# Second feed-forward input of a float32 decoder step: every second gate/up pair by seven half-token block products

## The chip, the core and the metric

The kernel runs as one program on one core of a Trainium2 chip. The metric is the device time of one execution in microseconds (us). TensorE (PE, with its weight loads as PEld), VectorE (DVE), ScalarE (ACT), GpSimd (POOL) and SyncE (SP, which issues the weight transfers) run side by side and wait for each other by semaphores.

## The reference

One layer of a hybrid recurrent decoder over 256 prompt tokens, 64 sample tokens and 16 meta tokens: a feed-forward block (FFN1), a token mixer with gated linear scans, and a second feed-forward block (FFN2). The part that matters here, cut from the reference:

```python
def swiglu(h, norm_w, w_in, w_out):
    u = rmsnorm(h, norm_w)
    g, up = jnp.split(u @ w_in, 2, axis=-1)      # w_in: 2048 x 11264
    return (jax.nn.silu(g) * up) @ w_out         # w_out: 5632 x 2048
...
    h = h + 0.5 * swiglu(h, ffn2_norm[l], w_ffn2_in[l], w_ffn2_out[l])
return rmsnorm(h, final_norm), ...
```

In FFN2 the meta tokens are gone: 320 tokens (`NO`) go through it.

## The kernel before

Activations lie transposed: 128 features in the partitions, tokens along the free dimension, `KT` = 16 feature tiles. Every large product is made of float32 numbers split in two parts: `uh` and `ul` (high and low part of the normalised input), and for each weight unit a high part `a` and a low part `b`. A unit is a 128x1024 piece of weights, eight 128x128 blocks. `stage` loads it (SP), casts it to the high part (ACT) and subtracts to get the low part (DVE); `mm3` then issues three matmuls for each block, a by uh, a by ul, b by uh, each over all 320 tokens into one PSUM bank. The high parts live in three buffers (`whp`), the low parts in three (`wlp`), the raw units in four (`rawp`), so that the staging of a unit waits for the matmuls of the unit three before it.

FFN2 (`ffn("f2", ...)`) has 44 gate/up pairs in 4 groups of 11. For one pair, `gin` calls `proj` twice (gate, up: 2 units, 48 matmuls each), then scales both by the norm factor `R`, applies the sigmoid and splits the product in `hh`, `hl`. `gout` multiplies a finished group by its part of `w_out`: 16 output tiles of two units (768 and 640 columns, 33 matmuls), each added to `h` by one DVE instruction. The order is that of the code, a group's `gin` and then the `gout` of the group before it; a scheduler then fixes one instruction order for each engine ahead of time, and each engine works through its own list in that order.

Of the kernel before, what the change touches and what calls it, by code (L numbers as in the profile page):

```python
# [20 lines left out]
NO = SEQ + NS  # L21
NT = NO + META
# [44 lines left out]
V_ALL = 100  # L67


def hybrid_step(tc, xT, w1i, w1a, w1b, win, wal, wup, wou, w2i, w2a, w2b, vec, cst_in, s0a, s0b,  # L70
                y, spa, spb, ssa, ssb):
    nc = tc.nc
    ctx = ExitStack()
    with ctx:
# [23 lines left out]
        def bank(tag, name, bufs):  # L98
            return psm.tile([P, 512], F32, tag=tag, name=name, bufs=bufs)

        def mmbank(name):
            return bank("mm", name, 3)

        def scbank(name):
            return bank("sc", name, 3)

        def stage(src, cols, name):
            r = rawp.tile([P, UNIT], F32, tag="raw", name="r" + name)
            nc.sync.dma_start(r[:, :cols], src)
# [157 lines left out]
        with ExitStack() as mx:  # L267
# [416 lines left out]
                advance()  # L684
            outpass(3, enter(V_N2, NO))

        def leave(m):
# [116 lines left out]
```

## Time and profile before

| | |
|---|---|
| time of three runs | 2563.48, 2564.34 (median), 2565.23 us |
| profiled execution, first to last instruction (span) | 2562.7 us |
| median less span | 1.6 us |
| PE, DVE, ACT busy over the span | 99%, 55%, 41% |
| FFN2 on PE: first matmul at 1617.77 us, the closing norm at 2547.57 us | 929.8 us |

A matmul's record is longer than the distance to the next, since matmuls are pipelined; how often PE starts one is read from the start times or from a stretch and its count. `idle before ... <-X` names what ended a wait.

### The profile page before, as it was taken

How to read it: one execution, taken by the hardware profiler on the slowest of the kernel's cores; microseconds unless marked ns; L12 is line 12 of the kernel's file. 1: busy time of each engine (PE TensorE's matmuls, PEld its weight loads, DVE VectorE, ACT ScalarE, POOL GpSimd, SP SyncE). 2: the span in 40 equal slices, each digit the busy share in tenths (PEclk: the TensorE clock that was granted, in tenths of full speed). 3: DMA queues.
4: the chain of work that ended last, by engine and by line, in shares of the span. 5: the costliest groups of instructions: out<-in, count | busy, mean ns of one | idle time of the engine just before them, and what ended most of it. 6: DMA issues, size and time to landing. Idle time of an engine off the chain costs nothing.

```text
span 2562.7 us, 43617 instructions
## 1 busy us (share of the span) xinstructions
PE 2539.0 (99%) x18086; PEld 2512.0 (98%) x18086; DVE 1421.3 (55%) x2395; ACT 1063.1 (41%) x1573; POOL 33.2 (1%) x65
## 2 busy tenths in 40 slices
PE   9999999999999999999999999999999999999997
PEld 8999999999999999999999999999999999999997
DVE  6454444444444456866757778655454554455454
ACT  6333333333333346555455456533333333333334
POOL 0000000000000000000000000000000000000000
PEclk9999999999999999999999999999999999999999
DMA  6444445444544444454444543544444544544453
GB/s 205 145 141 142 145 130 158 143 134 139 156 144 130 142 146 151 152 166 158 159 149 128 165 143 110 172 149 148 150 144 143 165 148 136 164 153 149 134 152 126
DMA packets 120247, 378.78 MB, mean 148 GB/s; under 512 B 13648, under 2 KB 16720, under 8 KB 120048
## 3 DMA queue, kind: packets, MB, share of 16 engines
q1 hardware_dynamic: 114176, 357.34, 45.5%
q0 software_dynamic: 5184, 17.83, 1.9%
q8 instruction: 141, 2.31, 0.4%
q10 hardware_dynamic: 688, 0.82, 0.1%
q14 instruction: 58, 0.48, 0.1%
HBM read 363.88 MB, written 12.06 MB: 147 GB/s over the span
## 4 chain that ended last, share of the span: by engine, by line
PE 59%; issue 38%; ACT 1%; DVE 1%; DMA 0%; SPq 0%; POOL 0%; POOLq 0%
PE po L124 4%; PE po L126 4%; PE po L125 4%; PE pf1u L125 4%; PE pf1g L125 4%; PE pf1g L124 4%; PE pf1u L124 4%; PE pf1g L126 4%; PE pf1u L126 4%; PE pw L124 1%; PE pw L125 1%; PE pw L126 1%; PE kv L505 1%; PE A L424 0%; PE st L124 0%
## 5 line engine op out<-in xcount | busy, mean ns | idle before, releaser
L125 PE MATMUL pf2u<-ul,af2u 128*128 128x320 f32 x704 | 218.3, 310 | 0.0
L125 PE MATMUL pf2g<-ul,af2g 128*128 128x320 f32 x704 | 218.3, 310 | 0.0
L124 PE MATMUL pf2u<-uh,af2u 128*128 128x320 f32 x704 | 217.5, 309 | 0.0
L124 PE MATMUL pf2g<-uh,af2g 128*128 128x320 f32 x704 | 217.3, 309 | 0.0
L126 PE MATMUL pf2u<-uh,bf2u 128*128 128x320 f32 x704 | 216.8, 308 | 0.0
L126 PE MATMUL pf2g<-uh,bf2g 128*128 128x320 f32 x704 | 216.8, 308 | 0.0
L124 PE MATMUL pf1g<-uh,af1g 128*128 128x336 f32 x672 | 212.9, 317 | 0.0
L125 PE MATMUL pf1u<-ul,af1u 128*128 128x336 f32 x672 | 212.8, 317 | 0.0
L125 PE MATMUL pf1g<-ul,af1g 128*128 128x336 f32 x672 | 212.8, 317 | 0.0
L124 PE MATMUL pf1u<-uh,af1u 128*128 128x336 f32 x672 | 212.7, 316 | 0.0
L126 PE MATMUL pf1g<-uh,bf1g 128*128 128x336 f32 x672 | 211.8, 315 | 0.0
L126 PE MATMUL pf1u<-uh,bf1u 128*128 128x336 f32 x672 | 211.8, 315 | 0.0
L111 ACT CAST af2g<-rf2g 128x1024 fp32r<-128x1024 f32 x88 | 92.3, 1049 | 192.9 <-PE pf2g L125 101.5
L111 ACT CAST af2u<-rf2u 128x1024 fp32r<-128x1024 f32 x88 | 92.3, 1049 | 184.2 <-PE pf2u L125 96.1
L111 ACT CAST af1g<-rf1g 128x1024 fp32r<-128x1024 f32 x84 | 88.1, 1048 | 193.7 <-PE pf1g L125 100.6
L111 ACT CAST af1u<-rf1u 128x1024 fp32r<-128x1024 f32 x84 | 88.1, 1049 | 192.3 <-PE pf1u L125 103.0
L113 DVE TENSOR_TENSOR bf2g<-rf2g,af2g 128x1024 fp32r<-128x1024 f32 x88 | 107.9, 1226 | 102.3 <-ACT af2g L111 102.3
L113 DVE TENSOR_TENSOR bf1g<-rf1g,af1g 128x1024 fp32r<-128x1024 f32 x84 | 103.0, 1226 | 100.6 <-ACT af1g L111 100.6
L113 DVE TENSOR_TENSOR bf2u<-rf2u,af2u 128x1024 fp32r<-128x1024 f32 x88 | 107.9, 1226 | 83.0 <-ACT af2u L111 83.0
L113 DVE TENSOR_TENSOR bf1u<-rf1u,af1u 128x1024 fp32r<-128x1024 f32 x84 | 103.0, 1226 | 87.9 <-ACT af1u L111 87.9
L126 PEld LDWEIGHTS pf2g<-uh,bf2g 128*128 128x128 f32 x704 | 132.5, 188 | 0.0
L126 PEld LDWEIGHTS pf2u<-uh,bf2u 128*128 128x128 f32 x704 | 132.5, 188 | 0.0
(1140 smaller groups left out, 7338.8 us busy)
## 6 DMA issues: line engine op xcount, KB each, us to landing
rf2g<-i_w2i SPq DMA_DIRECT2D x88, 512.0 KB, 3.6
rf2u<-i_w2i SPq DMA_DIRECT2D x88, 512.0 KB, 3.6
rf1g<-i_w1i SPq DMA_DIRECT2D x84, 512.0 KB, 3.6
rf1u<-i_w1i SPq DMA_DIRECT2D x84, 512.0 KB, 3.6
rw<-i_wou SPq DMA_DIRECT2D x32, 320.0 KB, 2.9
rw<-i_wou SPq DMA_DIRECT2D x12, 512.0 KB, 3.6
s<-i_s0a POOLq DMA_DIRECT2D x8, 512.0 KB, 4.8
s<-i_s0b POOLq DMA_DIRECT2D x8, 512.0 KB, 4.9
```

The costliest lines, as they stand in the source:

```text
L111: nc.scalar.copy(a[:, :cols], r[:, :cols])
L113: nc.vector.tensor_tensor(out=b[:, :cols], in0=r[:, :cols], in1=a[:, :cols].bitcast(F32), op=ALU.subtract)
L124: nc.tensor.matmul(ps, a[:, s], xh, start=(first and k == 0), stop=False)
L125: nc.tensor.matmul(ps, a[:, s], xl, start=False, stop=False)
L126: nc.tensor.matmul(ps, b[:, s], xh, start=False, stop=(last and k == n - 1))
L505: nc.tensor.matmul(kv, kk, vv, start=True, stop=True)
```

## The change

FFN2 gets a function of its own, `ffn2`, in place of `ffn`. 23 of the 44 pairs stay as they were (`plain`: the same 96 matmuls). The 21 odd pairs from 3 on (`SEVEN`) are computed by Strassen's algorithm on 2x2 blocks. The blocks of the input are even or odd feature tiles by first or second half of the tokens (160 each, `HO`), the blocks of the weights are gate or up by even or odd feature tiles, and seven products of sums of blocks take the place of eight products of blocks. Each product is eight times a matmul of `a` with high and low part of a half side by side (2 x 160 columns) and a matmul of `b` with the high part alone (160 columns). To allow that, `uh` and `ul` become interleaved halves of one tile `uhl`. `transform` makes the sums of input blocks (T0 to T3) once at the start of FFN2; `seven` loads four raw units r11, r12, r21, r22, forms the sums of weights on DVE, and collects the products in `m1`, `z`, `m7` and the PSUM tile `pa`. `raw` gives r21 and r22 two buffers of their own ("sraw", one each). `w_ffn2_in` is laid out on the host by even and odd tiles, `w_ffn2_out` by seven groups of 6, 6, 6, 6, 6, 7, 7 hidden tiles, and `gout` of the group before is now spread between the pairs, as one unit of 768 or 896 columns for an output tile.

```diff
+HO = NO // 2
+GROUPS2 = (6, 6, 6, 6, 6, 7, 7)
+GAT2 = [sum(GROUPS2[:g]) for g in range(len(GROUPS2) + 1)]
+SEVEN = {m for m in range(3, FT) if m % 2}
...
-        uh = cst.tile([P, KT, NT], F32R, name="uh")
-        ul = cst.tile([P, KT, NT], F32R, name="ul")
+        uhl = cst.tile([P, KT, 2, NT], F32R, name="uhl")
+        uh = uhl[:, :, 0]
+        ul = uhl[:, :, 1]
...
+        def ffn2(after):
...
+                def transform(i):
+                    e, o = 2 * i, 2 * i + 1
+                    we, wo = (v[:, V_N2 + k:V_N2 + k + 1] for k in (e, o))
+                    ta, tb, tc_ = (tmp.tile([P, NT], F32, tag=t, name="tf") for t in ("t0", "t1", "t2"))
+                    nc.vector.tensor_tensor(out=ta[:, t0], in0=h[:, e, t0], in1=h[:, e, t1], op=ALU.subtract)
+                    nc.scalar.activation(ta[:, t1], ta[:, t0], AF.Identity, scale=we)
+                    nc.scalar.activation(tc_[:, t0], h[:, o, t1], AF.Identity, scale=wo)
...
+                    for d, src, sg in ((0, ta[:, t1], 1.0), (1, tb[:, t0], -1.0), (3, tb[:, t1], -1.0),
+                                       (2, tc_[:, t1], -1.0)):
+                        nc.scalar.activation(T[d][:, i, 0], src, AF.Copy, scale=sg)
+                        nc.vector.scalar_tensor_tensor(out=T[d][:, i, 1], in0=src, scalar=sg,
+                                                       in1=T[d][:, i, 0].bitcast(F32), op0=ALU.mult, op1=ALU.subtract)
+
+                def cut(r, name):
+                    a = whp.tile([P, UNIT], F32R, tag="wh", name="a" + name)
+                    nc.scalar.copy(a, r)
+                    b = wlp.tile([P, UNIT], F32R, tag="wl", name="b" + name)
+                    nc.vector.tensor_tensor(out=b, in0=r, in1=a.bitcast(F32), op=ALU.subtract)
+                    return a, b
...
+                def prod(ps, ab, x, first, last):
+                    a, b = ab
+                    po = ps.rearrange("p (a t) -> p a t", a=2)
+                    for i in range(KT // 2):
+                        s = slice(i * P, (i + 1) * P)
+                        xi = x(i)
+                        nc.tensor.matmul(po, a[:, s], xi, start=(first and i == 0), stop=False, skip_group_check=True)
+                        nc.tensor.matmul(ps[:, t0], b[:, s], xi[:, 0], start=False, stop=(last and i == KT // 2 - 1), skip_group_check=True)
...
+                def seven(m, gs, us):
...
+                    r11 = raw(w2i[m, 0], "s11", rawp, "raw", 4)
+                    pa = bank("o", "pa", 2)[:, :NO]
+                    prod(pa, cut(r11, "s11"), B(0, t0), True, False)
+                    m1 = fac.tile([P, NO], F32, tag="m1", name="m1")
+                    nc.scalar.copy(m1, pa)
+                    r12 = raw(w2i[m, 1], "s12", rawp, "raw", 4)
+                    pb = scbank("pb")[:, :NO]
+                    prod(pb, cut(r12, "s12"), B(1, t0), True, True)
+                    nc.vector.tensor_tensor(out=m1, in0=pb, in1=m1, op=ALU.add)
+                    fold(gs[:, t0], m1)
+                    r21 = raw(w2i[m + 1, 0], "s21", fac, "sraw", 2)
+                    r22 = raw(w2i[m + 1, 1], "s22", fac, "sraw", 2)
+                    p1 = fac.tile([P, UNIT], F32, tag="sum", name="p1")
+                    nc.vector.tensor_tensor(out=p1, in0=r21, in1=r22, op=ALU.add)
+                    nc.vector.tensor_tensor(out=r21, in0=r21, in1=r11, op=ALU.add)
+                    nc.vector.tensor_tensor(out=r11, in0=p1, in1=r11, op=ALU.add)
+                    prod(pa, cut(r11, "s2"), X(1), False, False)
+                    z = fac.tile([P, NO], F32, tag="z", name="z")
+                    nc.scalar.copy(z, pa)
+                    pc = scbank("pc")[:, :NO]
+                    prod(pc, cut(r21, "s3"), X(2), True, False)
+                    m7 = fac.tile([P, NO], F32, tag="m7", name="m7")
+                    nc.scalar.copy(m7, pc)
+                    prod(pa, cut(p1, "s1"), X(0), False, False)
+                    nc.vector.tensor_tensor(out=m7, in0=pa, in1=m7, op=ALU.add)
+                    fold(us[:, t1], m7)
+                    prod(pc, cut(r22, "s22"), X(3), False, True)
+                    nc.vector.tensor_tensor(out=z, in0=pc, in1=z, op=ALU.add)
+                    fold(us[:, t0], z)
+                    nc.vector.tensor_tensor(out=r12, in0=r11, in1=r12, op=ALU.add)
+                    prod(pa, cut(r12, "s4"), B(1, t1), False, True)
+                    nc.vector.tensor_reduce(out=gs[:, t1], in_=pa.rearrange("p (a t) -> p t a", a=2), axis=AX.X,
+                                            op=ALU.add)
...
+                for g, n in enumerate(GROUPS2):
+                    for j in range(n):
+                        gin(g, j)
+                        if g == 0 and j < 2:
+                            for i in range(4 * j, 4 * j + 4):
+                                transform(i)
+                        if g:
+                            for m in range(KT * j // n, KT * (j + 1) // n):
+                                gout(g - 1, m)
+                for m in range(KT):
+                    gout(len(GROUPS2) - 1, m)
...
-        ffn("f2", w2i, w2a, w2b, NO, leave, None)
+        ffn2(leave)
```

The seven products of one pair are called here by the names of their weights, in the order in which PE makes them: s11, s12, s2, s3, s1, s22, s4.

**How it moves PE.** Before, PE's list within a gate tile of FFN2 reads as follows (`pf2g` is the PSUM tile, `af2g` and `bf2g` the two parts of the unit):

```order
L124 MATMUL pf2g_19408<-uh,af2g_0_19398 128x320
L125 MATMUL pf2g_19408<-ul,af2g_0_19398 128x320
L126 MATMUL pf2g_19408<-uh,bf2g_0_19400 128x320
L124 MATMUL pf2g_19408<-uh,af2g_0_19398 128x320
L125 MATMUL pf2g_19408<-ul,af2g_0_19398 128x320
L126 MATMUL pf2g_19408<-uh,bf2g_0_19400 128x320
```

In the changed kernel, the end of product s22 (into `pc`) and the start of s4 (into `pa`) of one pair of `SEVEN` read:

```order
L736 MATMUL pc_20264<-T3_17148,as22_20309 128x320
L737 MATMUL pc_20264<-T3_17148,bs22_20311 128x160
L736 MATMUL pc_20264<-T3_17148,as22_20309 128x320
L737 MATMUL pc_20264<-T3_17148,bs22_20311 128x160
L736 MATMUL pa_20186<-uhl_74,as4_20332 128x320 [waits DVE_49]
L737 MATMUL pa_20186<-uhl_74,bs4_20334 128x160
```

Three matmuls of 320 columns for a block of weights have become one of 320 and one of 160, 112 for a pair where there were 96, each with a weight block of its own; and s4 begins with a wait for DVE.

**How it moves DVE and SP.** On DVE, in the second half of a pair of `SEVEN`, there stands (`bs22`, `bs4` are the low parts that `cut` makes, `p1_20238` is the first sum of the next pair of `SEVEN`, made of its `rs21` and `rs22`, and `m7` reads `pa` once s1 is in it):

```order
L722 TENSOR_TENSOR bs22_19844<-rs22_19769,as22_19842 128x1024 [waits PE_49,Activation_49]
L722 TENSOR_TENSOR bs4_19867<-rs12_19742,as4_19865 128x1024 [waits PE_49,Activation_49]
L758 TENSOR_TENSOR p1_20238<-rs21_20234,rs22_20236 128x1024 [waits DMAHW6_49,DMAHW5_49,DVE_49]
L769 TENSOR_TENSOR m7_19818<-pa_19719,m7_19818 128x320 [waits PE_49,Activation_49]
L118 TENSOR_TENSOR bf2o1_2_19898<-rf2o1_2_19894,af2o1_2_19896 128x768 [waits DMAHW2_49,Activation_49]
L740 TENSOR_TENSOR us_19716<-m7_19818 128x160 [waits DVE_49]
L772 TENSOR_TENSOR z_19795<-pc_19797,z_19795 128x320 [waits PE_49]
```

On SP the two raw units of the next pair, `rs21` and `rs22`, stand among the loads that follow, each behind a wait for DVE:

```order
L114 DMA rf2o1_8_20361<-i_w2o 128x768 [waits DMAHW4_49,DVE_49]
L114 DMA rf2o1_9_20387<-i_w2o 128x768 [waits DMAHW5_49,DVE_49]
L114 DMA rf2g32_0_20416<-i_w2i 128x1024 [waits DVE_49]
L727 DMA rs21_20675<-i_w2i 128x1024 [waits DVE_49]
L727 DMA rs22_20677<-i_w2i 128x1024 [waits DVE_49]
L114 DMA rf2g32_1_20446<-i_w2i 128x1024 [waits DVE_49]
```

In the code, `p1` of the next pair comes more than a whole `plain` pair later than `m7`; the scheduler has put it ahead of `m7`. It does so in 20 of the 21 pairs (the last has no next). Before the change no DVE instruction of FFN2 used a unit that had not been cast by ACT first.

**How it moves DVE at the start of FFN2.** Between the first pairs DVE now makes the eight transforms; ahead of the third pair's first low part (`bf2g_0_17563`) there stand:

```order
L704 TENSOR_TENSOR tf<-h 128x160
L710 SCALAR_TENSOR_TENSOR tf<-h,v,tf 128x160 [waits Activation_49]
L803 TENSOR_TENSOR gs<-pf2g_17358,R 128x320 [waits DVE_49,PE_49]
L707 TENSOR_TENSOR tf<-tf 128x160 [waits Activation_49]
L715 SCALAR_TENSOR_TENSOR T_17147<-tf,T_17147 128x160 [waits Activation_49]
L708 SCALAR_TENSOR_TENSOR tf<-h,v,tf 128x160 [waits DVE_49]
L715 SCALAR_TENSOR_TENSOR T_17145<-tf,T_17145 128x160 [waits Activation_49]
L715 SCALAR_TENSOR_TENSOR T_17146<-tf,T_17146 128x160 [waits Activation_49]
L806 TENSOR_TENSOR gs<-gs,sg 128x320
L704 TENSOR_TENSOR tf<-h 128x160 [waits DVE_49]
L118 TENSOR_TENSOR bf2g_0_17563<-rf2g_0_17559,af2g_0_17561 128x1024 [waits DMAHW2_49]
```

Fourteen more instructions of 160 columns stand directly ahead of these, since the second pair's last low part; before the change the low part of the next unit followed there after two instructions of 320 columns at most.

## Rows read from the trace of the kernel before

**Rows 1.** The page: busy time, granted clock by slice, chain that ended last

```profile
span 2562.7 us, 43617 instructions
PE 2539.0 (99%) x18086; PEld 2512.0 (98%) x18086; DVE 1421.3 (55%) x2395; ACT 1063.1 (41%) x1573; POOL 33.2 (1%) x65
...
PEclk9999999999999999999999999999999999999999
...
PE 59%; issue 38%; ACT 1%; DVE 1%; DMA 0%; SPq 0%; POOL 0%; POOLq 0%
```

**Rows 2.** Busy time by engine in the stretch of FFN2

```profile
core 0: us, PE busy (x) PEld busy (x) DVE busy (x) ACT busy (x) POOL busy (x), PEclk, DMA share, GB/s
1617.77:2547.57 929.80, 929.80 (x6341) 929.64 (x6340) 465.22 (x606) 340.31 (x429) 0.00 (x0) 1.00 0.48 147
```

**Rows 3.** Waits in FFN2: who waited for whom, total us, times, longest

```profile
DVE bf2g L113 <- ACT af2g L111: 101.8, 86, 2.3
ACT af2g L111 <- PE pf2g L125: 101.5, 41, 2.5
```

**Rows 4.** Timeline (start us, length us): PE restarts after a wait, then runs steadily

```profile
1569.41 0.19 PEld L124 LDWEIGHTS pw<-oh,aw 128*128 128x128 f32 x1 [2.07 <-DVE h L670]
1569.41 0.42 PE L124 MATMUL pw<-oh,aw 128*128 128x320 f32 x1 [1.83 <-DVE h L670]
1569.52 0.19 PEld L125 LDWEIGHTS pw<-ol,aw 128*128 128x128 f32 x1
1569.67 0.31 PE L125 MATMUL pw<-ol,aw 128*128 128x320 f32 x1
1569.67 0.19 PEld L126 LDWEIGHTS pw<-oh,bw 128*128 128x128 f32 x1
1569.82 0.31 PE L126 MATMUL pw<-oh,bw 128*128 128x320 f32 x1
```

**Rows 5.** Weight loads by shape, whole span: busy us, mean ns of one

```profile
L126 PEld LDWEIGHTS pf2g<-uh,bf2g 128*128 128x128 f32 x704 | 132.5, 188 | 0.0
L424 PEld LDWEIGHTS A<-Q,K 128*32 128x32 f32 x960 | 12.8, 109 | 1.1 <-ACT ktok L415 1.0
```

**Rows 6.** DVE in FFN2 by line: busy us, mean ns of one, idle before

```profile
L113 DVE TENSOR_TENSOR bf2g<-rf2g,af2g 128x1024 fp32r<-128x1024 f32 x87 | 106.7, 1226 | 101.8 <-ACT af2g L111 101.8
L206 DVE SCALAR_TENSOR_TENSOR h<-po,h 128x320 f32<-128x320 f32 x63 | 31.0, 492 | 46.4 <-PE po L126 46.3
L141 DVE TENSOR_TENSOR hl<-us,hh 128x320 fp32r<-128x320 f32 x44 | 21.4, 486 | 0.0
L113 DVE TENSOR_TENSOR bf2o_9a<-rf2o_9a,af2o_9a 128x768 fp32r<-128x768 f32 x4 | 3.8, 958 | 0.9 <-ACT af2o_9a L111 0.9
```

**Rows 7.** ACT in FFN2 by line

```profile
L111 ACT CAST af2u<-rf2u 128x1024 fp32r<-128x1024 f32 x88 | 92.3, 1049 | 184.2 <-PE pf2u L125 96.1 <-PE pf2g L125 81.1 <-PE pf2u L126 2.8
L193 ACT ACTIVATE sg<-gs 128x320 f32<-128x320 f32 x44 | 20.6, 467 | 0.0
```

**Rows 8.** The raw units of the gate tiles: transfers and their time to landing

```profile
L109 SPq DMA_DIRECT2D rf2g<-i_w2i x88: 327/328/328, 1606.3 to 2363.4; - x88
...
DMA to landing us min/median/max: 3.3/3.6/5.1
```

**Rows 9.** Timeline of FFN2: hand-overs from PE to ACT, and from DVE to SP

```profile
1801.05 0.31 PE L125 MATMUL pf2u<-ul,af2u 128*128 128x320 f32 x1
...
1801.44 1.05 ACT L111 CAST af2u<-rf2u 128x1024 fp32r<-128x1024 f32 x1 [2.47 <-PE pf2u L125]
...
1802.52 1.23 DVE L113 TENSOR_TENSOR bf2u<-rf2u,af2u 128x1024 fp32r<-128x1024 f32 x1
...
1803.78 0.33 SPq L109 DMA_DIRECT2D rf2u<-i_w2i  x1
```

More of the change, by code (lines that the diff above doesn't have):

```diff
@@ L685, in hybrid_step, with raw, fold, plain @@
             outpass(3, enter(V_N2, NO))
+        def ffn2(after):
+            with ExitStack() as fx:
+                hidp = fx.enter_context(tc.tile_pool(name="hid2", bufs=2))
+                fac = fx.enter_context(tc.tile_pool(name="fac", bufs=1))
+                T = [fac.tile([P, KT // 2, 2, HO], F32R, name=f"T{i}") for i in range(4)]
+                hid = {}
+                t0, t1 = slice(0, HO), slice(HO, NO)
+                def transform(i):
[5 more added lines that the diff above has]
+                    nc.scalar.activation(tc_[:, t0], h[:, o, t1], AF.Identity, scale=wo)
+                    nc.vector.tensor_tensor(out=tb[:, t0], in0=tc_[:, t0], in1=ta[:, t1], op=ALU.add)
+                    nc.vector.scalar_tensor_tensor(out=tb[:, t1], in0=h[:, o, t0], scalar=wo, in1=tb[:, t0],
+                                                   op0=ALU.mult, op1=ALU.subtract)
+                    nc.vector.scalar_tensor_tensor(out=tc_[:, t1], in0=h[:, e, t1], scalar=we, in1=tc_[:, t0],
+                                                   op0=ALU.mult, op1=ALU.subtract)
+                    for d, src, sg in ((0, ta[:, t1], 1.0), (1, tb[:, t0], -1.0), (3, tb[:, t1], -1.0),
[9 more added lines that the diff above has]
+                    return a, b
+                def raw(src, name, pool, tag, bufs):
+                    r = pool.tile([P, UNIT], F32, tag=tag, name="r" + name, bufs=bufs)
+                    nc.sync.dma_start(r, src)
+                    return r
+                def prod(ps, ab, x, first, last):
[6 more added lines that the diff above has]
+                        nc.tensor.matmul(ps[:, t0], b[:, s], xi[:, 0], start=False, stop=(last and i == KT // 2 - 1), skip_group_check=True)
+                def fold(out, x):
+                    nc.vector.tensor_tensor(out=out, in0=x[:, t0], in1=x[:, t1], op=ALU.add)
+                def seven(m, gs, us):
+                    B = lambda q, t: (lambda i: uhl[:, 2 * i + q, :, t])
+                    X = lambda d: (lambda i: T[d][:, i])
+                    r11 = raw(w2i[m, 0], "s11", rawp, "raw", 4)
[31 more added lines that the diff above has]
+                                            op=ALU.add)
+                def plain(m, name):
+                    ps = mmbank("p" + name)[:, :NO]
+                    for q in range(2):
+                        un = stage(w2i[m, q], UNIT, f"{name}_{q}")
+                        mm3(ps, [(*un, 0, 8)], [(uh[:, k, :NO], ul[:, k, :NO]) for k in range(q, KT, 2)],
+                            first=(q == 0), last=(q == 1))
+                    return ps
+                def gin(g, j):
+                    if j == 0:
+                        hid[g] = [hidp.tile([P, max(GROUPS2), NO], F32R, tag=t, name=t) for t in ("hh", "hl")]
+                    jj = GAT2[g] + j
+                    gs = tmp.tile([P, NT], F32, tag="t0", name="gs")[:, :NO]
+                    us = tmp.tile([P, NT], F32, tag="t2", name="us")[:, :NO]
+                    sign = 1.0
+                    if jj in SEVEN:
+                        seven(2 * jj, gs, us)
+                        pg, pu, sign = gs, us, -1.0
+                    else:
+                        pg = plain(2 * jj, f"f2g{2 * jj}")
+                        if jj == 0:
+                            rstd(NO)
+                        pu = plain(2 * jj + 1, f"f2u{2 * jj}")
+                    sg = tmp.tile([P, NT], F32, tag="t1", name="sg")[:, :NO]
+                    nc.vector.tensor_tensor(out=gs, in0=pg, in1=R[:, :NO], op=ALU.mult)
+                    nc.scalar.activation(sg, gs, AF.Sigmoid)
+                    nc.vector.tensor_tensor(out=us, in0=pu, in1=R[:, :NO], op=ALU.mult)
+                    nc.vector.tensor_tensor(out=gs, in0=gs, in1=sg, op=ALU.mult)
+                    if sign > 0:
+                        nc.vector.tensor_tensor(out=us, in0=us, in1=gs, op=ALU.mult)
+                    else:
+                        nc.vector.scalar_tensor_tensor(out=us, in0=us, scalar=sign, in1=gs, op0=ALU.mult,
+                                                       op1=ALU.mult)
+                    hh, hl = hid[g]
+                    split(hh[:, j], hl[:, j], us)
+                def gout(g, m):
+                    n = GROUPS2[g]
+                    hh, hl = hid[g]
+                    at = KT * P * P * GAT2[g] + m * P * P * n
+                    un = stage(w2o[at:at + P * P * n].rearrange("(p c) -> p c", p=P), n * P, f"f2o{g}_{m}")
+                    ps = mmbank("po")[:, :NO]
+                    mm3(ps, [(*un, 0, n)], [(hh[:, j], hl[:, j]) for j in range(n)])
+                    nc.vector.scalar_tensor_tensor(out=h[:, m, :NO], in0=ps, scalar=0.5, in1=h[:, m, :NO],
+                                                   op0=ALU.mult, op1=ALU.add)
+                    if g == len(GROUPS2) - 1:
+                        after(m)
+                for g, n in enumerate(GROUPS2):
[9 more added lines that the diff above has]
+                    gout(len(GROUPS2) - 1, m)
@@ L769 @@
                           for i in range(len(PASSES)) for ms in pass_units(i)])
+    w2o = g["w_ffn2_out"][0].reshape(FT, P, KT, P)
+    w2o = np.concatenate([w2o[GAT2[i]:GAT2[i + 1]].transpose(2, 1, 0, 3).ravel() for i in range(len(GROUPS2))])
     s0a = g["state_hgrn"].reshape(NB, HA, P, P).transpose(1, 2, 0, 3)
```

8 lines of the change are left out of this document (4 added, 4 removed).

## Prediction

> **What bounds the kernel now.** The page first: PE is busy 99% of the span, the chain that ended last is PE and its issue for 97%, and the granted clock is full in every slice [rows 1], which is the 2.4 GHz level. Then the stretch of FFN2: 929.80 us hold 6341 matmuls, so PE starts one every 146.6 ns, while DVE is busy for 465 us and ACT for 340 us [rows 2]. The table of waits says the same from the other side: ACT's casts wait for PE to free a weight buffer and DVE waits for ACT [rows 3]; nobody keeps PE waiting. So FFN2 costs the number of matmuls times their distance, and work on DVE, ACT or the transfers costs nothing until it holds PE.
>
> **Seven products instead of eight: the matmuls.** A pair has 96 matmuls now, 96 x 0.1466 = 14.07 us. In a pair of `SEVEN` it has 56 of 320 columns and 56 of 160. By columns this is 7/8 of the work. What the distance of a 160-column matmul is depends on the weight load, since each matmul loads 128x128 weights of its own. Where PE restarts at 1569.41, the first load starts at 1569.41 and the next, which follows as soon as the first matmul has taken the weights over, at 1569.52; that first matmul's record is 0.42 us long instead of 0.31 [rows 4]. Both say that a load takes about 0.11 us at the full clock. The records of loads by width agree: 188 ns for 128 columns, 109 ns for 32 [rows 5], 79 ns for 96 more columns, 0.82 ns each, 105 ns for 128. In the steady part each load starts with the preceding matmul, at 1569.67 and 1569.82 [rows 4], so it lies behind it: a 0.147 us matmul hides a load of 0.11 us, and one of 160 columns does not.
>
> No row shows such a short matmul with these operands. Columns alone: 160/2.4 GHz is 67 ns, and 320 columns need 133 of their 146.6 ns, 13 ns over; so 80 ns is the lower end. The upper end is the load of 108 ns with the same 13 ns on top, 122 ns. I take 110 ns, the load itself, as the row nearest to the case. A product is then P = 8 x (0.1466 + 0.110) = 2.05 us, a pair 14.37 us: 0.30 us **more** than before, and 21 pairs cost **+6.2 us**. With 80 ns, P = 1.81 and the 21 pairs give 29.1 us back; with 122 ns, P = 2.15 and they cost 20.3 us.
>
> The Trainium skill speaks to this on the page "TensorE: Matmul & The Clock Gate" twice, and in two ways. Its section "Back-to-back issue gap" gives a warm gap of N/2.4 + 2.5 ns, 69 ns for 160 columns; by that P would be 1.73 us and the pairs would give back 42 us. Its section "LDWEIGHTS (loading the stationary operand)" gives columns/1.2, 107 ns for 128, which speaks against this change. The trace sides with the second: 0.11 us between the two loads [rows 4].
>
> **A wait that is added.** DVE's order shows, behind `bs4`, the sum `p1` of the next pair, and only then `m7`. `m7` reads `pa`, and PE's s4 writes to `pa` next, so all of PE's list waits for it. `p1` needs the next pair's r22, whose single buffer is this pair's r22 until `bs22` has read it. A walk from the moment s11 starts (products at 0, P, 2P ...):
> - s2 ends at 3P and frees the buffer for as22. PE's last reader in a unit starts at 1801.05 and ACT at 1801.44, 0.39 us later [rows 9]; that reader is here one pair of matmuls, 0.257 us, before 3P. ACT starts at 3P + 0.13 and casts for 1.049 us [rows 7].
> - `bs22` takes 1.226 us [rows 6] and ends at 3P + 2.44; SP issues the transfer 0.03 us after DVE's end (1802.52 + 1.23 and 1803.78, [rows 9]). A unit of 512 KB lands 3.6 us later [rows 8]: 3P + 6.07.
> - `p1` adds 1.226 us (the price of `bf2g`, the same size) and `m7` 0.49 us [rows 6]. s4 starts at about 3P + 7.85, hand-overs of 0.03 us each included.
>
> s4 was due at 6P. PE stands still for 7.85 - 3P = **1.69 us**, in 20 pairs (the last has no next): **+33.8 us**. Its ends: landing times of 3.3 and 5.1 us [rows 8] give 1.4 and 3.2 us; with P = 1.81 it is 2.4, with P = 2.15 it is 1.4, so what the matmuls gain the wait partly takes. Queued behind `p1` are also `z`, both folds and the first `bf2o`; they come late by the same 1.7 us, and PE wants the latter one product (2.05 us) after s4 starts, so nothing more is lost. On SP, the next gate unit stands behind r22 and comes 4 us late, but is needed only after two or three units of `gout` at 2.6 us each.
>
> **The start of FFN2.** The transforms are 64 DVE instructions of 160 columns. By width, 0.74 us more for 704 more columns [rows 6], one takes 0.32 us, with a scalar operand somewhat more; I take 0.36. DVE finishes the second pair's last low part at about 20.8 us after FFN2's first matmul (that pair's gate product ends at 21.1). Until the third pair's first low part come 22 of them, 0.98 us for two of 320 columns, 1.23 for the part itself: 30.9 us, where PE wants it at 28.2. That is a wait of 2.7. By the same count the first pair of `SEVEN` gets `bs11` at 49.4 where PE, now at 45.0, has waited 4.4, and `bs2`, which two sums precede, at 57.4 instead of 53.7, 3.7 more. Sum **+10.8 us**; below, nothing, if DVE runs further ahead, above, all 64 exposed, 23 us.
>
> **Added, and hidden.** A pair of `SEVEN` costs DVE seven cuts and four sums (11 x 1.23), seven PSUM reads, folds and the reduction (some 2.9 us) and the five that were there (2.45): 18.9 us instead of 7.4. With the plain pair's 7.4 and 5.3 output units (0.96 + 0.49 each) it is 34 us in a period in which PE needs 14.4 + 14.1 + 14.1 = 42.5: 80%, so DVE can follow. ACT's copies of `pa` and `pc` (0.47 us, [rows 7]) stand behind one cast of 1.05, together 1.5 us in the 2.05 us of the product between; without that cover each of the three copies would cost up to 0.5 us a pair. The 48 extra additions to `h` (24 us of DVE) lie behind PE's output units; bytes moved do not change; the end, 15 us after the last matmul, stays.
>
> **Sum.** +6.2 + 33.8 + 10.8 = +50.8 us on a span of 2562.7, that is 2613.5; the runs' median lies 1.6 us above the span: **2615 us**.
>
> **Rivals.**
> 1. *The load is hidden, the wait is paid* (80 ns): -29.1 + 20 x 2.41 + 10.8 = +30, **2594 us**. For it: a load may overlap more than one restart shows. Against: rows 4 and 5.
> 2. *Faster:* the same hidden load, and the joint at `pa` does not hold PE. Then -29.1 + 10.8 gives **2546 us**. It decides from a wait of under (29.1 - 10.8)/20 = 0.9 us a pair; the shortest landing, 3.3 us, still leaves 2.1 us there. The page's gap of 69 ns, with the wait of 7.85 - 5.18 = 2.67 us a pair, gives -42 + 53 + 11 = +22, 2587 us.
> 3. *The load bounds, the wait is absent* (the transfer is issued earlier than I walk it): +6.2 + 10.8, **2581 us**; without the start as well 2570.
> 4. *More joints are late:* DVE or ACT come into each pair behind, because the casts of s3, s22 and s4 and the copies share one queue with half a microsecond to spare. Another 1.0 us in each of 21 pairs and the whole 23 us at the start: **2648 us**.
>
> **Chances.** The forecast 0.60, rival 1 0.12, rival 2 0.07, rival 3 0.10, rival 4 0.11. The forecast's own range, from the ends of landing, load and start, is 2598 to 2632. The range of 2578 to 2636 adds rivals 1 and 3 and leaves out most of 2 and 4. A difference of 0.2%, 5 us, is about what a measurement of this kernel can tell: faster by more than that 0.07 (rival 2), within 0.02 (the low end of rival 3), slower 0.91.
>
> **What would show it.** In the changed profile a matmul of 160 columns followed by the next 0.11 us later (not 0.08); the weight loads back to back there; in each pair of `SEVEN` but the last an idle PE of 1.4 to 2 us ahead of s4, released by DVE's `m7`, and DVE idle ahead of `p1`, released by the transfer; FFN2 at about 981 us; idle PE of 2 to 5 us, two or three times, in its first 60 us. The forecast is wrong if s4 follows s22 without a gap, or if the distances are 0.08 us. PE stood for 1.83 us ahead of the restart at 1569.41 and went on at the full clock [rows 1, 4]; that it does so after the longer gaps at the start is an assumption.

## The result and the profile after

The changed kernel takes **2619.8 us** (median of four runs, 2616.7 to 2623.2) against 2563.9 us before (2563.1 to 2565.2): a ratio of **1.0218, 95% interval 1.0204 to 1.0233**. That is slower, as forecast, and 4.8 us above the 2615 us predicted. The profiled execution, the shortest of the four, has a span of 2614.9 us, 52.2 us more than before.

The page of the changed kernel, first lines and the engines' shares of the chain that ended last, answers to [rows 1]:

```profile
span 2614.9 us, 44858 instructions
PE 2560.1 (98%) x18422; PEld 2528.4 (97%) x18422; DVE 1669.3 (64%) x2785; ACT 1161.6 (44%) x1731; POOL 33.3 (1%) x65
...
PE 58%; issue 40%; ACT 1%; DVE 1%; DMA 0%; SPq 0%; POOL 0%; POOLq 0%
```

TensorE is still the bound. Busy time by stretch, the first row FFN2 from its first matmul to the first of the closing norm (compare [rows 2]); then two later stretches, and one like the first of these for comparison. PEclk is the granted clock as a share of 2.4 GHz:

```profile
core 0: us, PE busy (x) PEld busy (x) DVE busy (x) ACT busy (x) POOL busy (x), PEclk, DMA share, GB/s
1618.35:2599.82 981.47, 949.84 (x6676) 944.90 (x6675) 713.15 (x996) 437.90 (x587) 0.00 (x0) 0.99 0.47 140
...
1668.86:1675.69 6.83, 6.38 (x26) 6.38 (x27) 4.53 (x6) 2.07 (x3) 0.00 (x0) 0.50 0.47 156
1880.49:1883.90 3.41, 3.41 (x16) 3.41 (x16) 2.85 (x7) 0.62 (x1) 0.00 (x0) 0.50 0.65 172
...
1870.00:1876.83 6.83, 6.83 (x55) 6.83 (x54) 4.69 (x6) 4.43 (x6) 0.00 (x0) 1.00 0.65 182
```

FFN2 takes 981.47 us instead of 929.80 us, 51.7 more: all but half a microsecond of the difference lies there. Two of the rows show something that the prediction took not to happen, a clock of 0.50 (1.2 GHz) in the middle of FFN2.

The table of waits of FFN2 (who waited for whom, total us, times, longest), the rows that bear on the change:

```profile
DVE p L758 <- DMA rs<-i_w2i: 32.3, 20, 2.0
...
PE pa L736 <- DVE m L769: 28.7, 20, 1.8
PE pa L736 <- ACT as L720: 1.3, 1, 1.3
PE pa L737 <- DVE bs L722: 1.2, 1, 1.2
PE pf2g L131 <- DVE bf2g L118: 0.4, 1, 0.4
```

These are the two links of the predicted wait: `p1` waits for the transfer of r22, 20 times, and s4 waits for `m7`, 20 times. The remaining rows are the start of FFN2. The timeline of one joint (start us, length us; the pair's s11 began at 1865.77) shows the walk:

```profile
1873.14 1.23 DVE L722 TENSOR_TENSOR bs<-rs,as 128x1024 fp32r<-128x1024 f32 x1 [0.84 <-ACT as L720]
1874.40 0.33 SPq L727 DMA_DIRECT2D rs<-i_w2i  x1
...
1876.52 0.19 PEld L736 LDWEIGHTS pc<-T,as 128*128 128x128 f32 x1
1876.59 0.35 PE L736 MATMUL pc<-T,as 128*128 128x320 f32 x1
1876.62 0.19 PEld L737 LDWEIGHTS pc<-T,bs 128*128 128x128 f32 x1
1876.77 0.24 PE L737 MATMUL pc<-T,bs 128*128 128x160 f32 x1
1876.77 0.19 PEld L736 LDWEIGHTS pc<-T,as 128*128 128x128 f32 x1
1876.84 0.35 PE L736 MATMUL pc<-T,as 128*128 128x320 f32 x1
...
1878.06 0.24 PE L737 MATMUL pc<-T,bs 128*128 128x160 f32 x1
1878.12 1.23 DVE L758 TENSOR_TENSOR p<-rs,rs 128x1024 f32<-128x1024 f32 x1 [1.69 <-DMA rs<-i_w2i]
...
1879.27 0.49 DVE L769 TENSOR_TENSOR m<-pa,m 128x320 f32<-128x320 f32 x1
...
1879.81 0.42 PE L736 MATMUL pa<-uhl,as 128*128 128x320 f32 x1 [1.51 <-DVE m L769]
```

`bs22` ends at 1874.37, SP issues r22 of the next pair at 1874.40, it lands 3.72 us later, `p1` and then `m7` run, and s4 starts at 1879.81. The last matmul of s22 started at 1878.06; without a wait the next would have followed after 0.07 us, so TensorE lost 1.68 us. The waits table shows 1.51 because it counts from the end of the 0.24 us record. The 20 gaps, taken from start to start, are 0.45 us in the first pair and 1.52 to 2.03 us in the other 19, together 32.0 us after subtracting 0.073 us each. The matmul behind the first of s4 follows after 0.25 us instead of 0.185, another 1.4 us, so the waits cost 33.3 us.

The same rows show the pitch. A pair of matmuls (320 and 160 columns) repeats every 0.25 to 0.26 us (1876.59 and 1876.84); the median over all is 258 ns. Its two parts read as 185 and 73 ns, not as the 147 and 110 that the prediction described. A distance of some 0.08 us, which the prediction had named as a sign of being wrong, so stands in the record. The loads say why: the load behind the 160-column matmul starts with it, at 1876.77, and lasts about 0.10 to 0.11 us (as from 1876.52 to 1876.62), so the next matmul cannot have run before 1876.87; its record starts at 1876.84. So a record here begins while its weights are still on the way, and the wait shows inside the record of the longer matmul (0.35 us instead of 0.31). That reading was argued from one timeline; two experiments below test it.

### The profile page after: what moved, and what is told of

It is laid out like the page before. It is cut to its first block, busy times and chain, and to the rows that moved or that the text cites. A ratio compares the mean times of both kernels' runs of the same rounds, so it can differ in the third digit from the quotient of the medians.

```text
span 2614.9 us, 44858 instructions
## 1 busy us (share of the span) xinstructions
PE 2560.1 (98%) x18422; PEld 2528.4 (97%) x18422; DVE 1669.3 (64%) x2785; ACT 1161.6 (44%) x1731; POOL 33.3 (1%) x65
## 4 chain that ended last, share of the span: by engine, by line
PE 58%; issue 40%; ACT 1%; DVE 1%; DMA 0%; SPq 0%; POOL 0%; POOLq 0%
PE po L129 4%; PE po L131 4%; PE po L130 4%; PE pf1g L131 4%; PE pf1u L131 4%; PE pf1g L130 4%; PE pf1u L130 4%; PE pf1g L129 4%; PE pf1u L129 4%; PE pw L129 1%; PE pw L131 1%; PE pw L130 1%; PE kv L510 1%; PE A L429 0%; PE st L129 0%
## 5 line engine op out<-in xcount | busy, mean ns | idle before, releaser
L129 PE MATMUL po<-hh,af2o 128*128 128x320 f32 x704 | 218.3, 310 | 0.0
L130 PE MATMUL po<-hl,af2o 128*128 128x320 f32 x704 | 217.6, 309 | 0.0
L131 PE MATMUL po<-hh,bf2o 128*128 128x320 f32 x704 | 217.5, 309 | 0.0
L131 PE MATMUL pf1g<-uhl,bf1g 128*128 128x336 f32 x672 | 213.8, 318 | 0.0
L131 PE MATMUL pf1u<-uhl,bf1u 128*128 128x336 f32 x672 | 213.8, 318 | 0.0
L130 PE MATMUL pf1u<-uhl,af1u 128*128 128x336 f32 x672 | 212.4, 316 | 0.0
L130 PE MATMUL pf1g<-uhl,af1g 128*128 128x336 f32 x672 | 212.4, 316 | 0.0
L129 PE MATMUL pf1g<-uhl,af1g 128*128 128x336 f32 x672 | 212.2, 316 | 0.0
L129 PE MATMUL pf1u<-uhl,af1u 128*128 128x336 f32 x672 | 212.0, 315 | 0.0
L720 ACT CAST as<-rs 128x1024 fp32r<-128x1024 f32 x126 | 132.3, 1051 | 155.1 <-PE po L130 67.2
L722 DVE TENSOR_TENSOR bs<-rs,as 128x1024 fp32r<-128x1024 f32 x126 | 154.1, 1224 | 53.4 <-ACT as L720 53.4
L129 PEld LDWEIGHTS po<-hh,af2o 128*128 128x128 f32 x704 | 132.4, 188 | 0.0
```

The lines of the kernel that those rows point to most:

```text
L720: nc.scalar.copy(a, r)
L722: nc.vector.tensor_tensor(out=b, in0=r, in1=a.bitcast(F32), op=ALU.subtract)
```

## The experiments

Every kernel is compared with the kernel before on the same chip. The theory under test: the distance of a 160-column matmul is set by the weight load behind it, and s4 waits because `p1` stands ahead of `m7` and needs a transfer whose buffer comes free late.

**A control: the regrouping alone.** `SEVEN` is emptied and the transforms are left out; the new groups, layout and spread of the output units stay.

```diff
-SEVEN = {m for m in range(3, FT) if m % 2}
+SEVEN = set()
...
-                        if g == 0 and j < 2:
-                            for i in range(4 * j, 4 * j + 4):
-                                transform(i)
```

> Edit: SEVEN is empty and the transforms are gone; every pair is computed as before, but with the new tile uhl, the seven groups, and the output units spread between the pairs. Theory: all of the loss lies in the 21 pairs and their preparation; this kernel runs at 2565 us, within 0.2% of the kernel before, at 146.7 ns a matmul. Rival (regrouping costs): 112 additions to h instead of 64 and one unit instead of two for an output tile hold PE; then 5 to 15 us more than before.

Measured: 2568.96 us, ratio 1.0012 (1.0004 to 1.0021). FFN2 itself, its stretch in the table of busy time:

```profile
1619.10:2549.17 930.07, 930.07 (x6340) 929.91 (x6339) 485.40 (x638) 337.36 (x413) 0.00 (x0) 1.00 0.47 147
```

That is 930.07 us against 929.80 before. The regrouping costs FFN2 nothing; the cost is in the pairs. The median is 4.9 us above that of before and 4 above the expectation. This goes with the granted clock: four of the eleven executions lie at 2564.3 to 2566.1 us with a mean of 0.998, the profiled one among them, and seven at 2568.5 to 2569.5 us with 0.997. Where the clock fell in those seven no trace shows; the last section names a place ahead of FFN2 where it did in other kernels.

**The order of the scheduler: `m7` ahead of `p1`.**

```diff
+                    with ExitStack() as ord_:
+                        if m7s:
+                            ord_.enter_context(tc.issue_after(m7s[-1].ins))
                         nc.vector.tensor_tensor(out=p1, in0=r21, in1=r22, op=ALU.add)
...
-                    nc.vector.tensor_tensor(out=m7, in0=pa, in1=m7, op=ALU.add)
+                    m7s.append(nc.vector.tensor_tensor(out=m7, in0=pa, in1=m7, op=ALU.add))
```

> Edit: the first sum of the next pair, p1, is issued on DVE behind m7 instead of ahead of it; nothing else, the transfer and the buffers stay. Theory (queue order): the gap ahead of s4 vanishes in all 20 pairs (33 us), 2585 us, with DVE now idle ahead of p1 but nobody behind it who holds PE. The half clock just after some of these gaps should go as well, and with it the wider spread of the runs. Rival (another holder): the wait moves to the next joint, since z, the folds and the first low part of the output units queue behind p1; then PE waits at the first output unit instead and the time stays above 2610 us.

Measured: 2585.88 us, ratio 1.0083 (1.0068 to 1.0099), 34 us less than the changed kernel. All waits of TensorE in its FFN2:

```profile
PE pa L737 <- ACT as L721: 1.3, 1, 1.3
PE pa L738 <- DVE bs L723: 1.2, 1, 1.2
PE po L131 <- DVE bf2o L118: 0.6, 2, 0.4
PE pf2g L131 <- DVE bf2g L118: 0.3, 1, 0.3
```

No wait ahead of s4 is left: the place of `p1` in VectorE's list is what held TensorE. The half clock behind two of the gaps is gone as well; at the start 3.41 us of it remain. The profiled execution is still 22.3 us longer than that of before. Of these, 16.6 us lie in FFN2: some 7 are the matmuls' own, some 6 the start, and 3.4 are short waits in the output units. Most of these waits the table doesn't show, since it counts from the end of a matmul's record. The other 5.7 us lie ahead of FFN2, where the clock is at 0.50 for 6.83 us (last section).

**The transfer: r22 in a buffer that comes free earlier.** `p1` stays ahead of `m7`.

```diff
-GROUPS2 = (6, 6, 6, 6, 6, 7, 7)
+GROUPS2 = (6, 6, 6, 6, 5, 5, 5, 5)
...
-                    r22 = raw(w2i[m + 1, 1], "s22", fac, "sraw", 2)
+                    r22 = raw(w2i[m + 1, 1], "s22", fac, "sraw", 3)
```

(and the same 3 for r21).

> r21 and r22 share three buffers instead of two, and FFN2 has eight groups (6, 6, 6, 6, 5, 5, 5, 5) in place of seven, which makes the room; nothing else changes, and p1 of the next pair still stands ahead of m7 on VectorE, now even ahead of bs22. The next pair's r22 then takes the buffer that this pair's r21 leaves when bs3 has read it, one product earlier, so that its transfer is issued some 2 us sooner. Walk from the start of s11: landing at about 8.1 us, p1 done at 9.3, bs22 at 10.5, m7 as soon as s1 has ended, 12.3. My theory (p1 waits for the transfer, whose buffer comes free too late): the waits ahead of s4 fall from 1.7 to under 0.3 us in the pairs, and the time is that of the kernel with m7 ahead of p1: 2583 to 2592 us. The rival, that it is the place of p1 ahead of m7 by itself, its 1.2 us on VectorE, that holds TensorE: the waits stay above 1 us, 2605 us or more. One group of output units more costs some 16 matmuls of an eviction each on VectorE and no TensorE time.

Measured: 2598.55 us, ratio 1.0128 (1.0113 to 1.0144), between the two expectations. The largest row of its waits in FFN2:

```profile
PE pc L737 <- DVE bs L722: 10.7, 14, 1.6
```

The wait ahead of s4 is gone, as the theory says, but one has appeared a product earlier, at the first matmul of s22 with b. `p1` now stands ahead of `bs22` as well and still waits for the transfer: it starts 8.1 to 9.9 us after s11 in all pairs but the first, `bs22` is done some 2.4 us after that, at 10.5 to 12.2, and s22 wants it at 5P + 0.2 = 10.5. My expectation asked only for s4's time. The rival, that `p1`'s own 1.2 us hold s4, falls. The cause has two halves: the transfer is late, and what is queued behind `p1` decides who pays.

**The a matmuls first.** In each product the eight matmuls with `a`, then the eight with `b`.

```diff
                         nc.tensor.matmul(po, a[:, s], xi, start=(first and i == 0), stop=False, skip_group_check=True)
-                        nc.tensor.matmul(ps[:, t0], b[:, s], xi[:, 0], start=False, stop=(last and i == KT // 2 - 1), skip_group_check=True)
+                    for i in range(KT // 2):
+                        s = slice(i * P, (i + 1) * P)
+                        nc.tensor.matmul(ps[:, t0], b[:, s], x(i)[:, 0], start=False, stop=(last and i == KT // 2 - 1), skip_group_check=True)
```

> Edit: within a product all eight matmuls by the high part come first, then the eight by the low part; the same matmuls, the same columns, another order. Theory (weight load): a matmul behind one of 160 columns waits for its 128 columns of weights, 0.11 us. Then the distances come apart: 147 ns from a 320-column matmul to the next, 110 to 112 ns from a 160-column matmul to the next; the product stays at 2.06 us. Rival (form): the 320-column matmul of two halves itself takes 185 ns, as its row reads in the changed kernel, and the one of 160 columns 73 ns by its columns; then these two distances stay as they are in the new order. Both give the same length of a product. By the walk of the wait, the buffer of the high part of s2 is free 0.9 us sooner, so that DVE's cut of s22 ends some 1.0 us sooner and the gap ahead of s4 shrinks from 1.7 to about 0.7 us: time about 2600 us. If the gap is not made by the chain cut of s22, transfer, p1, m7, it stays at 1.7 us and the time at 2620 us.

Measured: 2605.13 us, ratio 1.0161 (1.0147 to 1.0175). A stretch of its timeline, a product at a time:

```profile
2053.69 1.02 PE L739 MATMUL pa<-T,bs 128*128 128x160 f32 x8
2054.54 1.38 PE L736 MATMUL pc<-T,as 128*128 128x320 f32 x8
2055.76 1.02 PE L739 MATMUL pc<-T,bs 128*128 128x160 f32 x8
2057.54 1.44 PE L736 MATMUL pa<-uhl,as 128*128 128x320 f32 x8 [0.76 <-DVE m L771]
```

Between themselves the 160-column matmuls are a median of 111 ns apart, the 320-column ones 147: this is the load, read without any neighbour of another width. Only the first distance of each eight differs, 75 ns and 187 ns, as the recorded 73 and 185 do in the changed kernel. The product does not get shorter (1.22 + 0.85 us), but `a` is let go 1 us earlier, the transfer starts earlier, and the gaps ahead of s4 shrink to 0.7 to 1.1 us but for three longer ones. The walk of the prediction holds when one of its inputs is moved; the time is 5 us above the one expected.

**Both orders together,** `m7` first and a first:

> Both earlier edits together: m7 ahead of the next pair's p1 on VectorE, and in each product the eight matmuls with a first, then the eight with b. If the order of the matmuls saves time only by letting go of the a buffer earlier (my reading of the run with a first), nothing is left to gain once the wait ahead of s4 is gone: a matmul of a every 147 ns, of b every 111 ns, 14.45 us a pair as before, the time within 3 us of the kernel with m7 first alone, 2583 to 2589 us. The rival, that alternating wide and narrow matmuls costs something by itself, gives 2570 to 2580 us.

Measured: 2580.78 us, ratio 1.0064 (1.0050 to 1.0077), 2 us under the lower end and 5 us less than `m7` first alone. The 21 pairs take 305.6 us instead of 307.7, but the first of them alone has 16.8 instead of 19.4: its waits are shorter and the clock stays full there. A later pair has 14.44 instead of 14.42, so the matmuls gain nothing. The output units take 310.5 us instead of 313.1. Here the scheduler put the first `bf2o` ahead of `p1`, which the edit did not intend, and `p1` waits 1.0 us in all for its transfer instead of 24.3; which of the two saves the 2.6 us was not separated.

**Is it the load, and which one?** First more columns for the matmul with `b`: 232 instead of 160 in four of the seven products (the 72 columns more read on into the low part of the input, a product that is otherwise left out).

```diff
-                        nc.tensor.matmul(ps[:, t0], b[:, s], xi[:, 0], start=False, stop=(last and i == KT // 2 - 1), skip_group_check=True)
+                        nc.tensor.matmul(ps[:, c], b[:, s], xb, start=False, stop=(last and i == KT // 2 - 1), skip_group_check=True)
```

> Edit: in the four products on T (s2, s3, s1, s22) the matmul by the low part runs over 232 columns instead of 160, taking the first 72 columns of the low half with it, 45% more columns in 672 matmuls. Theory (weight load): the next matmul waits for its weights anyway, so the sum of a 320-column matmul and this one stays at 258 ns (at most 262) and the time within 5 us of the changed kernel, 2620 us. Rival (columns or form decide): 72 columns more at 2.4 GHz are 30 ns more for each, 288 ns the sum, 4.8 products of 8 a pair: 672 x 30 ns = 20 us more, 2640 us, less what the gap ahead of s4 takes back (three of the four lie ahead of its chain's end, some 0.7 us a pair, so at least 2626 us).

Measured: 2618.89 us, ratio 1.0214 (1.0200 to 1.0228). 45% more columns are free: the pair of matmuls stays at 258 ns, now read as 152 and 106.

Then, on top of `m7` first, short weight blocks: 32 of 128 columns for `b`, and in another kernel for `a`.

```diff
-                        nc.tensor.matmul(ps[:, t0], b[:, s], xi[:, 0], start=False, stop=(last and i == KT // 2 - 1), skip_group_check=True)
+                        sb = slice(i * P, i * P + P // 4)
+                        nc.tensor.matmul(ps[:P // 4, t0], b[:, sb], xi[:, 0], start=False, stop=(last and i == KT // 2 - 1), skip_group_check=True)
```

> On top of the kernel with m7 first: in each product the matmuls with b use only the first 32 of the 128 columns of their weight block, so that the b part of three quarters of the output features is left out; the moving side stays at 160 columns, the matmuls with a stay whole. It makes the weight load of b short (a quarter of the columns) and leaves that of a. My theory: the load that is exposed is that of the next matmul with a, since it has to fit behind the short matmul with b. Then nothing changes: 258 ns for a pair of matmuls, 2583 to 2589 us. The rival, as the recorded distances would have it (185 ns from a to b, 73 from b to a): the load of b itself is exposed behind a; then a pair of matmuls takes 147 + 73 to 80 = 220 to 227 ns and the time is 2545 to 2555 us.

```diff
-                        nc.tensor.matmul(po, a[:, s], xi, start=(first and i == 0), stop=False, skip_group_check=True)
+                        w = P if first and i == 0 else P // 4
+                        nc.tensor.matmul(po[:w], a[:, i * P:i * P + w], xi, start=(first and i == 0), stop=False, skip_group_check=True)
```

> The mirror of the run with short b: the matmuls with a use only the first 32 of the 128 columns of their weight block (all but the first of an accumulation, which stays whole), so that the a part of three quarters of the output features is left out; those with b stay whole. Now the load that has to fit behind the 160-column matmul is a quarter as long. My theory: that matmul is then bound by its columns alone, 80 ns at most, a pair of matmuls takes 220 to 230 ns, a product 1.8 us, and the 1176 pairs of matmuls save some 33 to 45 us: 2541 to 2555 us, faster than the kernel before, or up to 10 us more where the staging of the units no longer follows the shorter products. The rival gives no change, 2583 to 2589 us.

Measured: short b 2583.97 us, ratio 1.0078 (1.0061 to 1.0095), no change; short a 2568.01 us, ratio 1.0014 (1.0005 to 1.0024), 18 us less than `m7` first but 3 us above the upper end expected. Loads of the first kernel, matmuls and loads of the second:

```profile
1907.69 0.19 PEld L737 LDWEIGHTS pa<-T,as 128*128 128x128 f32 x1
1907.80 0.11 PEld L739 LDWEIGHTS pa<-T,bs 128*32 128x32 f32 x1
1907.95 0.19 PEld L737 LDWEIGHTS pa<-T,as 128*128 128x128 f32 x1
```

```profile
1905.02 0.24 PE L739 MATMUL pa<-T,bs 128*128 128x160 f32 x1
1905.02 0.11 PEld L738 LDWEIGHTS pa<-T,as 128*32 128x32 f32 x1
1905.10 0.31 PE L738 MATMUL pa<-T,as 128*32 128x320 f32 x1
1905.10 0.19 PEld L739 LDWEIGHTS pa<-T,bs 128*128 128x128 f32 x1
1905.24 0.24 PE L739 MATMUL pa<-T,bs 128*128 128x160 f32 x1
```

With short `a` the distances are 148 and 73 ns, and a pair of `SEVEN` takes 12.42 us instead of 14.42. So the exposed load is that of the next `a`, behind the 160-column matmul, although the recorded 185 and 73 had pointed at `b`; a load of 0.11 us costs 36 ns a block, 2.0 us a pair. The 21 pairs take 266.8 us instead of 307.7, 41 us less. Only 18 of the 41 us reach the time. The waits of short a, and VectorE at one of them:

```profile
PE po L131 <- DVE bf2o L118: 19.4, 18, 1.7
PE pf2g L131 <- DVE bf2g L118: 3.0, 3, 1.5
```

```profile
1911.89 1.23 DVE L763 TENSOR_TENSOR p<-rs,rs 128x1024 f32<-128x1024 f32 x1 [1.72 <-DMA rs<-i_w2i]
1913.04 0.32 DVE L742 TENSOR_TENSOR us<-m 128x160 f32<-128x160 f32 x1
1913.27 0.95 DVE L118 TENSOR_TENSOR bf2o<-rf2o,af2o 128x768 fp32r<-128x768 f32 x1
```

It is the same transfer again: the pair ends 2.0 us earlier, `p1` starts only some 0.8 us earlier because it still waits for r22, and now the first output unit queued behind it is late. In each of its three places, ahead of `m7`, of `bs22` and of `bf2o`, `p1` handed its wait to the next instruction in the list.

**The start.** On top of `m7` first:

```diff
-SEVEN = {m for m in range(3, FT) if m % 2}
+SEVEN = {m for m in range(7, FT) if m % 2}
...
-                        if g == 0 and j < 2:
-                            for i in range(4 * j, 4 * j + 4):
+                        if g == 0 and j < 4:
+                            for i in range(2 * j, 2 * j + 2):
```

> On top of the kernel with m7 first: the seven-product pairs begin with the eighth pair instead of the fourth (19 instead of 21), and the transforms are spread over the first four pairs, two in each, instead of four in each of the first two. My reading of the start: the waits of 0.4 to 1.6 us ahead of the third and fourth pair (3.4 us in all) come from transforms that VectorE has to finish first, and the half-clock stretch just behind them from these waits; with half as many transforms between two pairs VectorE keeps ahead, both vanish, and two seven-product pairs fewer save 0.6 us. Expected 2577 to 2581 us, that is 5 to 8 us under the kernel with m7 first. The rival, that the half-clock stretch and the waits come with the first seven-product pair itself, wherever it stands: they reappear at the eighth pair, and the time stays at 2583 to 2587 us.

Measured: 2579.04 us, ratio 1.0054 (1.0042 to 1.0067), 7 us less than `m7` first, as expected. The waits at the start are gone, none appears at the eighth pair, and the clock is full throughout FFN2.

**A version that the runs point to.** Two facts together: a 160-column matmul costs 111 ns, and 232 columns cost no more. So the low parts don't belong in half-width products. If the high parts are cut on a common grid, their sums are exact, the seven products need high parts alone, and the low parts can be multiplied plainly over 320 columns.

```diff
+                    nc.scalar.activation(t, r, AF.Identity, bias=grid[:, 0:1])
+                    nc.scalar.activation(a, t, AF.Identity, bias=grid[:, 1:2])
...
+                    for i in range(KT // 2):
+                        nc.tensor.matmul(po, a[:, i * P:(i + 1) * P], x(i), start=(first and i == 0),
...
+                def low(ps, b, q):
+                    for i in range(KT // 2):
+                        nc.tensor.matmul(ps, b[:, i * P:(i + 1) * P], uh[:, 2 * i + q, :NO], start=(q == 0 and i == 0),
```

> A version drawn from the runs so far: no matmul of 160 columns is left. The high part of every weight unit is cut on one common grid (a multiple of 2 to the power of -13), so that the sums of high parts are exact and go to TensorE as they are; the seven products are made of high parts alone, eight matmuls of 2x160 columns each, and the low parts of the four units are multiplied plainly, eight matmuls of 320 columns each, into two banks of their own that are added at the end. A pair has 56 + 32 = 88 matmuls, all 147 ns apart, 12.9 us instead of the 14.07 us of a plain pair. 20 pairs from the sixth on, the transforms spread over the first four pairs, nine groups of output units (for room). VectorE does four low parts and four sums in a pair instead of seven and four, ScalarE eight passes instead of seven. If the load behind the 160-column matmul was what made the seven products dearer, and TensorE stays the bound, the 20 pairs give back 23 us: 2540 to 2549 us, faster than the kernel before. The rival, that VectorE or ScalarE no longer follow the shorter pairs (as VectorE did not in the run with short a), leaves a wait of 1 us or more in each pair: 2560 to 2575 us.

Measured: **2552.74 us, ratio 0.9955 (0.9941 to 0.9969)**: faster than both kernels, by less than expected. Its FFN2 and the waits of TensorE there:

```profile
1622.19:2535.35 913.16, 910.04 (x6180) 906.89 (x6178) 658.81 (x1026) 472.59 (x633) 0.14 (x2) 1.00 0.49 150
```

```profile
PE pa L742 <- DVE p L736: 1.9, 5, 0.6
PE pc L742 <- DVE p L736: 1.1, 1, 1.1
```

The 20 pairs take 264.6 us, 13.2 each instead of 14.07, and give back 16.8 us of the 23 expected. Nearly all of the rest are waits, 5.9 us from start to start: eight of 0.25 to 1.2 us and some two dozen shorter ones. Those that the table shows are for a sum of weights. The matmuls themselves stay 147 ns apart, those of 2x160 columns too. In the profiled run FFN2 also starts 4.4 us later than in [rows 2]; from 1571.04 to 1577.87 the granted clock was 0.50 there.

## Why the prediction was right, and where its sum was off

- **The matmuls** (+6.2 predicted): a pair of `SEVEN` without a wait takes 14.42 us (the kernel with `m7` first), 302.8 us for 21, against 21 x 14.07 = 295.5, **+7.3**. Its two matmuls take 257.5 ns, predicted 256.6. That it is the load of the next weights is shown by the runs with a first, wide b, short b and short a. Rivals 1 and 2, which hide the load, fall. On the Trainium skill's page "TensorE: Matmul & The Clock Gate", the section "LDWEIGHTS (loading the stationary operand)" gives 107 ns, and the 111 ns of the run with a first agree. The Trainium skill's section "Back-to-back issue gap" there calls the gap behind the 69 ns that of an isolated matmul and says that it under-counts at small N, so the two sections do not differ as the prediction has it. Here 73 ns come with a short pair (148 and 73) only where the load behind is short.
- **The wait ahead of s4** (+33.8): **+33.3**, in 20 pairs, by the links that the walk named. The run with `m7` first takes it away and leaves rival 3's case, forecast at 2581 and measured at 2585.9. That is near by parts that differ: its FFN2 has 16.6 us more than before where rival 3 has 17.0, but with half the start, 3.4 us in the output units, and 5.7 us more ahead of FFN2.
- **The start** (+10.8): **+3.6**, that is 0.5, 0.25 and 2.9 us where 2.7, 4.4 and 3.7 were forecast. This term was mis-sized. The step "one takes 0.32 us, with a scalar operand somewhat more; I take 0.36" took records for distances. VectorE in the changed kernel, ahead of the third pair:

```profile
1637.09 0.32 DVE L707 TENSOR_TENSOR tf<-tf 128x160 f32<-128x160 f32 x1
1637.32 0.38 DVE L710 SCALAR_TENSOR_TENSOR tf<-h,v,tf 128x160 f32<-128x160 f32 x1
1637.62 0.38 DVE L708 SCALAR_TENSOR_TENSOR tf<-h,v,tf 128x160 f32<-128x160 f32 x1
```

  The records are as long as estimated, but the next instruction starts 0.08 us before a record ends: the distances are 0.23 and 0.30 us. From the second pair's last low part to the end of the third pair's first one the prediction counts 10.1 us (22 transforms, two of 320 columns, the part itself); the trace has 7.4. Over 64 transforms the difference is some 5 us, by this estimate most of the error.
- **The clock** (assumed full after waits): **about +6.3**, not in the sum. In the stretch at 1880.49 a pair of matmuls takes 0.48 us instead of 0.258, so 3.41 us lose 1.6; the stretch at 2365.18 is alike, and that of 6.83 us at 1668.86, in part a wait, holds 14 such pairs and loses 3.1. The prediction's last sentence called the full clock after the longer gaps an assumption; it failed at the start of FFN2 and after two of the 20 gaps ahead of s4.
- Together 7.3 + 33.3 + 3.6 + 6.3 = 50.5 of the 51.7 us; the remaining 1.2 lie in plain and output matmuls, at a mean of 147.2 ns instead of 146.7. The start, too high by 7.2, and the clock, missing by 6.3, nearly cancelled. That FFN2 came out at 981.5 us where about 981 were forecast is luck in these two terms; the matmuls and the wait were right by themselves.
- **Added, and hidden**: right. The control shows that regrouping, output units and additions to `h` cost FFN2 nothing. With `m7` first the joints other than the start wait 3.4 us in all, in the output units, where rival 4 has 1.0 us in each of 21 pairs.

## What to carry to other kernels

Count an algorithm that saves multiplications in matmuls at their real distance: a narrow matmul that brings its own weights costs the load of the weights behind it, so seven eighths of the columns were more time here, and the same algorithm paid, by 0.45%, once every matmul was wide. In a list that is worked through in order, look for the instruction that needs a transfer and ask what stands behind it; moving the buffer alone, or the instruction alone, may hand the wait to a neighbour. Take throughput from start to start, not from the length of records, on VectorE as on TensorE.

## What the runs showed of the hardware that was not expected

- **TensorE's clock fell after waits that had left it full elsewhere.** At 1879.81 it restarted after a wait of 1.5 us by the record, ran 0.68 us and fell to 1.2 GHz for 3.41 us; one other of the 19 gaps of 1.5 to 2.0 us ended so, 17 did not. Ahead of FFN2, in code that the two kernels below share, TensorE waited 1.84 us in both; it is the restart that [rows 4] shows for the kernel before. With a and `m7` first the clock fell 0.8 us after the restart and stayed at half for 6.83 us; in the changed kernel it stayed full:

```profile
1571.35 0.41 PE L129 MATMUL pw<-oh,aw 128*128 128x320 f32 x1 [1.84 <-DVE h L675]
...
1572.13:1578.96 6.83, 6.83 (x39) 5.86 (x38) 3.78 (x8) 3.70 (x11) 0.00 (x0) 0.50 0.16 50
```

```profile
1569.99 0.41 PE L129 MATMUL pw<-oh,aw 128*128 128x320 f32 x1 [1.84 <-DVE h L675]
...
1572.13:1578.96 6.83, 6.83 (x47) 6.55 (x48) 5.93 (x13) 4.46 (x15) 0.32 (x1) 1.00 0.41 107
```

  The first of these runs reached FFN2 at 1622.7 us, the second at 1618.4. In the traces kept, the clock fell there with a first, r22 in another buffer, `m7` first, both orders, the late start (for 3.41 us) and the last version, and stayed full in the others, so differences of up to 5 us between two of these times need not be the edit's. What decides it from one execution to the next stays open.
- **A recorded start of a matmul can lie ahead of the end of its weight load.** The distances 185 and 73 ns put the cost on the wrong matmul of the two; only their sum, or a run with one load shortened, tells.
